# A pooling mixer worked out behind the half groups of a projection, and loads issued from GpSimd's queue, in a two-layer decoder trunk

## The chip, the core and the metric

The kernel runs on one core of one Trainium2 chip. The metric is the device time of one execution in microseconds (us). Below, PE is TensorE, DVE is VectorE, ACT is ScalarE, POOL is GpSimd and SP is SyncE, whose queue issues transfers; L564 is line 564 of the kernel before. The change adds lines, so that the same statement has a number some 3 to 9 higher in the changed kernel (L564 is L567 there, L878 is L881).

## The reference, cut to what matters

Two layers work on 256 tokens of width 2048. A vector c gives, per layer, six sections of conditioning (shift, scale and gate for the mixer and for the feed-forward part), each 2048 wide. Layer 0 has one input projection that feeds an attention with a window and a pooling mixer; both outputs go into one output projection, and a gated feed-forward part follows.

```python
c_act = silu(c)
mod = c_act @ ada_w[layer] + ada_b[layer]          # 6 sections of 2048
h = rms_norm(x, norm_mix_pre) * (1 + sc_m) + sh_m
q, k, v, p = split(h @ w_in)                       # layer 0
a = sliding_window_attention(q, k, v, sinks)
# pooling mixer, 4 groups of 256 channels, windows 2, 4, 8, 16
d = trailing_mean(p, win) - p
bo = (einsum('btgc,gcd->btgd', d, pool_w) + pool_b) * pool_scale
y = concat([a, bo]) @ w_out
x = x + gt_m * rms_norm(y, norm_mix_post)
h = rms_norm(x, norm_ffn_pre) * (1 + sc_f) + sh_f
y = (gelu(conv(h @ w_up_gate)) * (h @ w_up)) @ w_down
x = x + gt_f * rms_norm(y, norm_ffn_post)
```

## The kernel before, in words

All weights stream from memory in pieces of 1 MB. A piece is loaded into one of three slots tagged "w"; ACT copies it, rounded, into an upper half (`whi`, L303), DVE subtracts to get the lower half (`wlo`, L304), each in two instructions of 128x1024, and PE multiplies in three passes (upper by upper, upper by lower, lower by upper: `mm3`, L339 to L341).

The conditioning is worked out in between, in blocks of 128 channels. Blocks of the tables `ada_m` and `ada_dve` take one 1 MB load and one DVE instruction each (L564, a multiply with `c_row` summed along the row, and the short L565). The gate of the mixer (`ada_g`) takes 16 loads and four PE instructions each (L547). The loads of `ada_pe` and `ada_m` alternate between two slots tagged "a" and the "w" slots; all `ada_g` and `ada_dve` loads go to "a" slots. In the kernel before, every load of either tag is issued from SP's queue.

Who does a block when is set by the object `behind` with the generator `ada_gate` (16 steps) followed by the 144 blocks of `ada_dve`. `push()` does one step. `step()` is called with every `load_split` and pushes `pace` steps on average; `PACE_0` sets the pace over the eight parts of the first output projection (two loads each). `need(l, s, b)` pushes until block b of section s is done; it is called by `norm.scale`, which needs the shift and the scale of four channel blocks at a time. The order of `ada_dve` is shift and scale of the feed-forward part of layer 0 block by block, then its gate, then layer 1.

Layer 0 runs so:

- `first_of_all` (L406) does the input projection in four quarters of the inner dimension; in each, five groups of weights (`EV_ORDER`), each with two half groups of 24 matmuls (h = 0, 1). Groups 0 and 1 stay in PSUM; the half groups of groups 2 to 4 are added up in SBUF (`held`, L434). The next quarter's blocks of `ada_m` are pushed by `between`.
- `even_layer` (from L886) then makes keys and queries and works out the pooling mixer: `pool_tile` (L857) forms window sums on DVE, `pool_group` (L874) multiplies by `pool_w` on PE (L878) and scales on DVE (L881). After each of the four groups, `POOL_PUSH` pushes two steps of `behind`, 8 in all. One step of attention (`next(att)`) comes after the first group.
- The output projection runs in two halves, first over the mixer's channels, then over the attention's. The attention is a filler of the first half.
- The feed-forward part starts with `first_halves` (L437): 24 column tiles in two sets of three weight groups; quarters 0 and 1 of the first set, then quarters 0 to 3 of the second set (each group in a quarter is a part of 48 matmuls), then the rest of the first set. `norm.scale` is called ahead of each of the four quarters. After each part, `half_way` pushes one step while fewer than `ADA_0` = 48 are done. The pace of `step()` is 0 here.

An order of instructions on each engine is set by a scheduler at build time, and each engine then runs its own list in order.

Of the kernel before, what the change touches and what calls it, by code (L numbers as in the profile page):

```python
# [38 lines left out]
MARKED = 4  # L39
QUIET = 1  # L40
PACE_0 = (2, 2, 2, 2, 1.5, 1, 1, 0.5)
POOL_PUSH = (2, 2, 2, 2)
EV_ORDER = (0, 1, 2, 3, 4), (3, 4, 2, 0, 1)
ADA_PACE = (0.65, 0.35, 0.2)
SH_M, SC_M, GT_M, SH_F, SC_F, GT_F = range(6)
# [133 lines left out]
def trunk(ctx: ExitStack, tc: tile.TileContext, A, out):  # L179
    nc = tc.nc  # L180
# [113 lines left out]
    behind = Behind()  # L294


    def load(src, shape=(128, NK, 128), tag="w"):
        w = wst.tile(list(shape), F32, name="w", tag=tag, bufs=SLOTS[tag == "a"])
        nc.sync.dma_start(w, src)
        return w  # L300

    def split(src, hi, lo):
# [100 lines left out]
                        between(q, 4 * g + i // 4)  # L403
        return PS

    def first_of_all(norm, between):  # L406


        fixed = [bank((128, 2, T)) for _ in range(4)]
        held = [granule() for _ in range(6)]  # L410
        for q in range(4):
            norm.scale(slice(4 * q, 4 * q + 4))
            for k in range(4 * q, 4 * q + 4):
                norm.tile(k)
            for n, g in enumerate(EV_ORDER[q == 3]):
                W = load_split(A["ev_first"][q, g])
                for h in range(2):
                    stay = g < 2
                    ps = fixed[2 * g + h] if stay else bank((128, 2, T))
                    for k in range(4):  # L420
                        act = norm.tile(4 * q + k)
                        for j in range(2):
                            flags = (k == 0 and j == 0 and not (stay and q), k == 3 and not (stay and q < 3))
                            if (g, h) == (4, 1):
                                mm3(ps[:, j, :], tok(act, j), W(8 + 2 * k, 2), *flags, skip_group_check=True)
                            else:
                                mm3(ps[:, j, :], W(8 * h + 4 * j + k), act, *flags, skip_group_check=True)
                        between(q, 8 * n + 4 * h + k)
                    if not stay:
                        to = held[2 * g - 4 + h]  # L430
                        if q == 0:
                            nc.scalar.activation(to, ps, AF.Copy)
                        else:
                            nc.vector.tensor_tensor(to, ps, to, op=OP.add)  # L434
        return [t[:, j, :] for t in fixed + held for j in range(2)], held[5]
# [391 lines left out]
    def new_mix():  # L827
        M = {}

        def mix(k):  # L830
            if k not in M:
                g = granule(F32R)
                M[k] = g[:, 0, :], g[:, 1, :]
            return M[k]
        return mix
# [48 lines left out]
    def even_layer():  # L884
# [20 lines left out]
        def between(q, g):  # L905
            if q < 3 and g in EARLY:
                next(quarters[q + 1])
            if q < 3 and g == 39:
                drain(quarters[q + 1])
        PS, v = first_of_all(norm, between)  # L910
        kz = key_halves(PS[0:2])
        Q = Copies()
        Q = [Q.copy(ps, scale=q_scale[:, t:t + 1]) for t, ps in enumerate(PS[2:8])]
        for t, ps in enumerate(PS[8:10]):
            nc.scalar.activation(ps, ps, AF.Copy, scale=q_scale[:, 6 + t:7 + t])
            Q.append(ps)
        rec = pool_consts()
        pw = load(A["pool_w"], (128, 4, 2, 256))
        mix = new_mix()
        behind.pace = PACE_0[0]  # L920
        att = behind.fill(attention(Q, kz, v, distances(True), lambda h: sm("sinks", h), lambda t: mix(8 + t)))
        for g in range(4):
            pool_group(g, [pool_tile(g, PS[10 + 2 * g + e], rec) for e in range(2)], pw, mix)
            if g == 0:
                next(att)
            for _ in range(POOL_PUSH[g]):
                behind.push()
        post = Post(0, GT_M, "norm_mix_post0", "up_first0", Norm(0, SC_F, SH_F, "norm_ffn_pre0"))
        for half in range(2):
            if half:  # L930
# [272 lines left out]
```

## Time and profile before

| | us |
|---|---|
| median of 3 runs | 2221.96 |
| lowest and highest run | 2221.46 and 2225.73 |
| the profiled execution's own time | 2221.93 |
| its span | 2220.2 |
| PE busy in it | 2143.8 (97%) |
| DVE busy in it | 1686.2 (76%) |

The span is what the profile records, and the execution's own time is 1.7 us longer. PE is busy for 97% of the span, and the chain of work that ended last lies on PE for 90% of it. PE's time with nothing running is 76 us in all. A busy PE is not one at its peak: an isolated matmul shows its whole length, while back to back matmuls overlap.

### The profile page before, as it was taken

What the parts mean: (1) busy time and instruction counts of PE and PEld (TensorE: products, weight loads), DVE (VectorE), ACT (ScalarE), POOL (GpSimd) and SP (SyncE); (2) the same over time, 40 slices, a digit from 0 to 9 for tenths busy, and PEclk for the clock granted to TensorE, in tenths of its full rate; (3) what the DMA queues carried; (4) which work ended last, traced back from release to release, by engine and by line L of the source; (5) the groups of instructions that cost most, each with busy time, mean ns of one, the idle gap of its engine ahead of it and who ended that gap; (6) DMA issues with size and microseconds to landing.
All of it is one profiled execution on the core that took longest, in us unless ns stands there. A gap on an engine that the chain in (4) does not pass through costs nothing.

```text
span 2220.2 us, 31418 instructions
## 1 busy us (share of the span) xinstructions
PE 2143.8 (97%) x12390; PEld 1857.7 (84%) x12390; DVE 1686.2 (76%) x2533; ACT 1153.6 (52%) x1790; POOL 10.4 (0%) x48
## 2 busy tenths in 40 slices
PE   7888998999999999999899999989999999999998
PEld 5886677997888888888797898878888888888886
DVE  4896798898899899887799867579955665665566
ACT  3345655464555455445576655555545544554453
POOL 1000000000000000000000000000000000000000
PEclk8899998999999999999999999989999999999999
DMA  9987886889889888887387635558855555555553
GB/s 372 348 334 280 322 339 258 328 310 350 308 325 341 331 322 332 330 332 263 135 300 275 229 132 190 190 189 307 319 209 184 188 197 189 190 188 194 188 190 114
DMA packets 81373, 578.42 MB, mean 261 GB/s; under 512 B 9156, under 2 KB 9156, under 8 KB 11464
## 3 DMA queue, kind: packets, MB, share of 16 engines
q1 hardware_dynamic: 81224, 576.40, 70.5%
q8 instruction: 97, 1.59, 0.3%
q14 instruction: 52, 0.43, 0.1%
HBM read 574.27 MB, written 2.10 MB: 260 GB/s over the span
## 4 chain that ended last, share of the span: by engine, by line
PE 90%; DVE 6%; ACT 2%; DMA 1%; issue 1%; SPq 0%; DVEq 0%; ACTq 0%
PE ps L358 28%; PE ps L361 15%; PE ps L340 14%; PE ps L339 14%; PE ps L341 14%; DVE w L564 2%; DVE wlo L304 2%; ACT g L582 1%; PE ps L758 1%; PE ps L547 1%; ACT whi L303 0%; PE ps L795 0%; PE ps L805 0%; DVE x L696 0%; DMA x<-in_x_dram 0%
## 5 line engine op out<-in xcount | busy, mean ns | idle before, releaser
L304 DVE TENSOR_TENSOR wlo<-w,whi 128x1024 fp32r<-128x1024 f32 (+1 forms) x706 | 847.7, 1218 | 314.9 <-PE ps L340 155.6
L303 ACT ACTIVATE whi<-w 128x1024 fp32r<-128x1024 f32 (+1 forms) x706 | 737.4, 1055 | 587.0 <-PE ps L341 281.4
L358 PE MATMUL ps<-g,whi 128*128 128x512 f32 x2736 | 654.4, 391 | 0.0
L358 PEld LDWEIGHTS ps<-g,whi 128*128 128x128 f32 x2736 | 501.9, 188 | 100.5 <-issue 1.2
L340 PE MATMUL ps<-wlo,g 128*128 128x512 f32 (+1 forms) x1152 | 429.1, 373 | 2.2 <-DVE wlo L304 2.2
L339 PE MATMUL ps<-whi,g 128*128 128x512 f32 (+1 forms) x1152 | 428.8, 373 | 0.3 <-ACT g L303 0.2
L341 PE MATMUL ps<-whi,g 128*128 128x512 f32 (+1 forms) x1152 | 428.2, 372 | 0.6 <-DVE g L304 0.6
L564 DVE SCALAR_TENSOR_TENSOR w<-w,c_row 128x2048 f32<-128x2048 f32 x168 | 383.7, 2285 | 3.9 <-DMA w<-in_ada_dve_dram 3.8
L361 PEld LDWEIGHTS ps<-g,wlo 128*128 128x128 f32 x2736 | 350.5, 191 | 13.6
L361 PE MATMUL ps<-g,wlo 128*128 128x256 f32 x2736 | 354.9, 283 | 0.0
L340 PEld LDWEIGHTS ps<-wlo,g 128*128 128x128 f32 x1152 | 217.1, 188 | 42.9 <-DVE wlo L304 4.0
L339 PEld LDWEIGHTS ps<-whi,g 128*128 128x128 f32 x1152 | 216.9, 188 | 40.5 <-issue 1.9
L341 PEld LDWEIGHTS ps<-whi,g 128*128 128x128 f32 x1152 | 216.9, 188 | 38.7 <-DVE g L304 1.5
L339 PE MATMUL ps<-g,whi 128*128 128x256 f32 x800 | 234.9, 297 | 13.7 <-ACT whi L303 7.1
L340 PE MATMUL ps<-g,whi 128*128 128x256 f32 x800 | 235.0, 295 | 0.3 <-DVE g L630 0.3
L341 PE MATMUL ps<-g,wlo 128*128 128x256 f32 x800 | 231.3, 294 | 1.4 <-DVE wlo L304 1.3
L339 PEld LDWEIGHTS ps<-g,whi 128*128 128x128 f32 x800 | 161.2, 203 | 17.3 <-ACT whi L303 8.7
L340 PEld LDWEIGHTS ps<-g,whi 128*128 128x128 f32 x800 | 161.8, 202 | 2.4 <-DVE g L630 2.3
L341 PEld LDWEIGHTS ps<-g,wlo 128*128 128x128 f32 x800 | 160.4, 202 | 2.4 <-DVE wlo L304 2.0
L366 ACT ACTIVATE low<-ps 128x256 f32<-128x256 f32 x156 | 59.5, 381 | 94.8 <-PE ps L361 94.4
L1133 DVE SCALAR_TENSOR_TENSOR z<-low,smalls,z 128x255 f32<-128x255 f32 (+1 forms) x148 | 71.3, 482 | 25.1 <-ACT z L1131 23.5
L1131 ACT ACTIVATE z<-low,smalls 128x256 f32<-128x256 f32 x74 | 44.6, 602 | 84.5 <-DVE low L367 84.5
(195 smaller groups left out, 1173.8 us busy)
## 6 DMA issues: line engine op xcount, KB each, us to landing
w<-in_up_dram SPq DMA_DIRECT2D x148, 1024.0 KB, 4.8
w<-in_ada_dve_dram SPq DMA_DIRECT2D x144, 1024.0 KB, 6.9
w<-in_down_dram SPq DMA_DIRECT2D x88, 1024.0 KB, 4.8
w<-in_up_first_dram SPq DMA_DIRECT2D x28, 1024.0 KB, 7.7
w<-in_ada_m_dram SPq DMA_DIRECT2D x24, 1024.0 KB, 7.5
w<-in_ev_first_dram SPq DMA_DIRECT2D x20, 1024.0 KB, 7.1
w<-in_ada_g_dram SPq DMA_DIRECT2D x16, 1024.0 KB, 4.8
w<-in_ev_out_dram SPq DMA_DIRECT2D x16, 1024.0 KB, 7.8
```

The costliest lines, as they stand in the source:

```text
L303: nc.scalar.activation(hi, src, AF.Copy)
L304: nc.vector.tensor_tensor(lo, src, hi.bitcast(F32), op=OP.subtract)
L339: nc.tensor.matmul(ps, lh, rh, start=first, stop=False, **kw)
L340: nc.tensor.matmul(ps, lh, rl, start=False, stop=False, **kw)
L341: nc.tensor.matmul(ps, ll, rh, start=False, stop=last, **kw)
L358: nc.tensor.matmul(self.ps.rearrange("p a b -> p (a b)"), w(k)[0], act(k).both, start=k == 0, stop=False, skip_group_check=True)
L361: nc.tensor.matmul(self.ps[:, 0, :], w(k)[1], act(k)[0], start=False, stop=k == NK - 1, skip_group_check=True)
L366: nc.scalar.activation(low, self.ps[:, 1, :], AF.Copy)
L547: nc.tensor.matmul(ps[32 * j:32 * j + 32, :], c_rep[:, k, :], w[:, 0, 512 * j:512 * j + 512], start=k == 0, stop=k == NK - 1, tile_positio ...
L564: nc.vector.scalar_tensor_tensor(w, w, 1.0, c_row, op0=OP.mult, op1=OP.mult, accum_out=m)
L1131: nc.scalar.activation(z, pg, AF.Identity, scale=cw(2, f), bias=sm(f"ffn_b{l}", f))
L1133: nc.vector.scalar_tensor_tensor(z[:, lag:], pg[:, :T - lag], cw(2 - lag, f), z[:, lag:], op0=OP.mult, op1=OP.add)
```

## The change

The pooling mixer is worked out inside the last quarter of `first_of_all`: after every half group but the first two a callback `pools` does one `pool_tile`, and after every second one the `pool_group` of the group that came before; the groups come in the order 1, 2, 3, 0, and group 0's `pool_group` comes after the projection. `POOL_PUSH` and its 8 pushes are gone, and nothing takes their place. Every load with tag "a" is issued from GpSimd's queue. `pool_w` is loaded into an "a" slot instead of a "w" slot.

```diff
-POOL_PUSH = (2, 2, 2, 2)
+POOL_ORDER = (1, 2, 3, 0)
...
         w = wst.tile(list(shape), F32, name="w", tag=tag, bufs=SLOTS[tag == "a"])
-        nc.sync.dma_start(w, src)
+        (nc.gpsimd if tag == "a" else nc.sync).dma_start(w, src)
...
-    def first_of_all(norm, between):
+    def first_of_all(norm, between, done):
...
                         between(q, 8 * n + 4 * h + k)
+                    if q == 3 and n:
+                        done(2 * n + h - 2, held)
...
-        PS, v = first_of_all(norm, between)
+        rec = pool_consts()
+        mix = new_mix()
+        pw, ds = [], {}
+
+        def pools(i, held):
+            if i == 0:
+                pw.append(load(A["pool_w"], (128, 4, 2, 256), "a"))
+            g, e = POOL_ORDER[i // 2], i % 2
+            t = 2 + 2 * g + e
+            ds.setdefault(g, []).append(pool_tile(g, held[t // 2][:, t % 2, :], rec))
+            if e == 0 and i:
+                last = POOL_ORDER[i // 2 - 1]
+                pool_group(last, ds[last], pw[0], mix)
+        PS, v = first_of_all(norm, between, pools)
...
-        rec = pool_consts()
-        pw = load(A["pool_w"], (128, 4, 2, 256))
-        mix = new_mix()
+        pool_group(POOL_ORDER[3], ds[POOL_ORDER[3]], pw[0], mix)
         behind.pace = PACE_0[0]
         att = behind.fill(attention(...))
-        for g in range(4):
-            pool_group(g, [pool_tile(g, PS[10 + 2 * g + e], rec) for e in range(2)], pw, mix)
-            if g == 0:
-                next(att)
-            for _ in range(POOL_PUSH[g]):
-                behind.push()
+        next(att)
```

What the scheduler makes of it shows in the lists of the engines. First PE, at the end of the projection, before (`ps_342` is the projection's last bank, L878 the mixer, L757 and L758 the first attention scores, L547 the gate's blocks):

```order
L340 MATMUL ps_342<-g_1492,whi_1745 128x256
L341 MATMUL ps_342<-g_1492,wlo_1746 128x256
L878 MATMUL ps_1855<-pdiff_1842,w_1824 128x256
L878 MATMUL ps_1855<-pdiff_1851,w_1824 128x256
L878 MATMUL ps_1863<-pdiff_1842,w_1824 128x256
L878 MATMUL ps_1863<-pdiff_1851,w_1824 128x256
L757 MATMUL ps_1871<-g_1797,g_1805 128x128
L758 MATMUL ps_1871<-g_1797,g_1805 128x256
L757 MATMUL ps_1886<-g_1797,g_1805 128x128
L758 MATMUL ps_1886<-g_1797,g_1805 128x256
L547 MATMUL ps_1901<-w_1902,c_rep_78 32x512 x4
L547 MATMUL ps_1901<-w_1908,c_rep_78 32x512 x4
```

The same place in the changed kernel (L881 is the mixer, L760 and L761 the scores, L550 the gate's blocks, L798 the transposes of the attention's weights):

```order
L340 MATMUL ps_350<-g_1500,whi_1865 128x256
L341 MATMUL ps_350<-g_1500,wlo_1866 128x256
L881 MATMUL ps_1970<-pdiff_1898,w_1600 128x256
L881 MATMUL ps_1978<-pdiff_1898,w_1600 128x256
L760 MATMUL ps_1997<-g_1951,g_1959 128x128
L761 MATMUL ps_1997<-g_1951,g_1959 128x256
L881 MATMUL ps_1970<-pdiff_1947,w_1600 128x256
L881 MATMUL ps_1978<-pdiff_1947,w_1600 128x256
L760 MATMUL ps_2012<-g_1951,g_1959 128x128
L761 MATMUL ps_2012<-g_1951,g_1959 128x256
L550 MATMUL ps_2042<-w_2043,c_rep_78 32x512 x4
L798 MATMUL ps_2055<-ident_93,p_2000 128x128
```

Twelve of the sixteen mixer matmuls now stand between the projection's matmuls, and four behind them; two steps of the gate stand between the first scores and the output projection, where eight stood.

Second DVE, in the feed-forward part, ahead of the casts (L629, L632) of the second quarter's activations. Before, from the third conditioning block after the first quarter's casts:

```order
L564 SCALAR_TENSOR_TENSOR w_3486,mod04_124<-w_3486,c_row_79 128x2048
L304 TENSOR_TENSOR wlo_3530<-w_3527,whi_3529 128x1024
L565 TENSOR_TENSOR mod04_124<-mod04_124,smalls_76 128x1
L304 TENSOR_TENSOR wlo_3534<-w_3527,whi_3533 128x1024
L564 SCALAR_TENSOR_TENSOR w_3585,mod03_123<-w_3585,c_row_79 128x2048
L565 TENSOR_TENSOR mod03_123<-mod03_123,smalls_76 128x1
L304 TENSOR_TENSOR wlo_3592<-w_3589,whi_3591 128x1024
L629 CAST g_3500<-h_3498 128x256
L629 CAST g_3508<-h_3506 128x256
```

In the changed kernel, from the fifth block on (L608 makes the scale `s` that the casts' input waits for):

```order
L567 SCALAR_TENSOR_TENSOR w_3462,mod04_124<-w_3462,c_row_79 128x2048
L304 TENSOR_TENSOR wlo_3584<-w_3577,whi_3583 128x1024
L568 TENSOR_TENSOR mod04_124<-mod04_124,smalls_76 128x1
L567 SCALAR_TENSOR_TENSOR w_3466,mod03_123<-w_3466,c_row_79 128x2048
L304 TENSOR_TENSOR wlo_3642<-w_3639,whi_3641 128x1024
L568 TENSOR_TENSOR mod03_123<-mod03_123,smalls_76 128x1
L567 SCALAR_TENSOR_TENSOR w_3470,mod04_124<-w_3470,c_row_79 128x2048
L568 TENSOR_TENSOR mod04_124<-mod04_124,smalls_76 128x1
L608 SCALAR_TENSOR_TENSOR s_2028<-mod04_124,smalls_76 128x4
L632 CAST g_3488<-h_3486 128x256
L567 SCALAR_TENSOR_TENSOR w_3474,mod03_123<-w_3474,c_row_79 128x2048
L633 TENSOR_TENSOR g_3488<-h_3486,g_3488 128x256
```

Four blocks and eight lower halves stand between the first casts of quarters 0 and 1 before, seven blocks and ten lower halves in the changed kernel, an eighth block stands behind the first cast, and the scale `s` stands behind the seventh.

Third POOL, in the first 200 us; a piece of the difference, with - before and + in the changed kernel (L860 and L863 clear the pads of the window sums, L748 and L751 clear the tiles of the keys):

```order
 L239 AFFINE_SELECT dist<-dist 128x256
-L860 MEMSET pd 128x16
+L299 DMA w<-in_ada_pe_dram 128x2048
 L242 AFFINE_SELECT dist<-dist 128x256
-L748 MEMSET g 128x512 x2
-L860 MEMSET pd 128x16 x7
+L299 DMA w<-in_ada_m_dram 128x2048 x12
+L299 DMA w<-in_pool_w_dram 128x2048
+L299 DMA w<-in_ada_g_dram 128x2048
+L863 MEMSET pd 128x16 x7
+L751 MEMSET g 128x512 x2
+L299 DMA w<-in_ada_g_dram 128x2048 x15
```

The clears stand behind loads that wait for a free slot, and later in the list `pool_w`'s slot has to be free for the gate's second load.

## Rows read from the trace of the kernel before

**Rows 1.** The page, busy time of each engine: share of the span, instructions.

```profile
PE 2143.8 (97%) x12390; PEld 1857.7 (84%) x12390; DVE 1686.2 (76%) x2533; ACT 1153.6 (52%) x1790; POOL 10.4 (0%) x48
```

**Rows 2.** Busy time by stretch: us, busy and count by engine, PE clock, DMA share, GB/s.

```profile
core 0: us, PE busy (x) PEld busy (x) DVE busy (x) ACT busy (x) POOL busy (x), PEclk, DMA share, GB/s
35.00:153.00 118.00, 103.64 (x742) 100.06 (x742) 104.85 (x140) 43.29 (x55) 0.00 (x0) 0.88 0.91 350
...
215.50:287.00 71.50, 70.19 (x383) 48.36 (x382) 49.85 (x138) 47.54 (x132) 1.90 (x4) 1.00 0.86 323
```

**Rows 3.** Timeline of PE from the projection's end to the output projection's start.

```profile
185.11 0.28 PE L340 MATMUL ps<-g,whi 128*128 128x256 f32 x1
185.23 0.28 PE L341 MATMUL ps<-g,wlo 128*128 128x256 f32 x1
185.35 1.89 PE L878 MATMUL ps<-pdiff,w 128*128 128x256 f32 x8
187.08 0.38 PE L757 MATMUL ps<-g 128*128 128x128 f32 x2
...
192.63 1.25 PE L878 MATMUL ps<-pdiff,w 128*128 128x256 f32 x4 [2.22 <-DVE pdiff L871]
...
213.69 1.06 PE L547 MATMUL ps<-w,c_rep 128*32 128x512 f32 x8
214.69 0.66 PE L805 MATMUL ps<-pt,g 128*64 128x256 f32 x4
...
215.50 0.50 PE L339 MATMUL ps<-whi,g 128*128 128x512 f32 x1
```

**Rows 4.** Busy time by stretch, from the first cast to the fourth quarter's.

```profile
352.75:447.81 95.06, 92.74 (x743) 90.83 (x742) 80.85 (x106) 43.31 (x56) 0.00 (x0) 0.98 0.83 324
```

**Rows 5.** Waits of SP's queue over the span: us in total, times, longest.

```profile
SPq L299 <- DVE mod L565: 157.0, 38, 9.9
SPq L299 <- DVE w L564: 133.2, 42, 6.7
```

**Rows 6.** Waits of DVE from 35 to 153 us, same columns.

```profile
DVE wlo L304 <- ACT whi L303: 7.4, 3, 2.7
DVE g L434 <- PE ps L341: 4.7, 5, 1.1
```

**Rows 7.** The gate's blocks, L547, from 185 to 216 us: count, ns min/median/max.

```profile
L547 PE MATMUL ps<-w,c_rep x64: 592/617/1062, 188.5 to 214.2; 128*32 128x512 f32 x64
```

**Rows 8.** Timeline of ACT, the last scaling of the first attention weights.

```profile
195.23 0.80 ACT L781 ACTIVATE p<-p,st 128x128 f32<-128x128 f32 x2 [0.18 <-DVE st L776]
```

**Rows 9.** The page, transfers: count, size, median us from issue to landing.

```profile
w<-in_ada_dve_dram SPq DMA_DIRECT2D x144, 1024.0 KB, 6.9
```

**Rows 10.** Timeline of DVE in the feed-forward part's first quarters.

```profile
367.53 1.22 DVE L304 TENSOR_TENSOR wlo<-w,whi 128x1024 fp32r<-128x1024 f32 x1
368.67 0.15 DVE L565 TENSOR_TENSOR mod<-mod,smalls 128x1 f32<-128x1 f32 x1
368.74 1.22 DVE L304 TENSOR_TENSOR wlo<-w,whi 128x1024 fp32r<-128x1024 f32 x1
369.87 2.29 DVE L564 SCALAR_TENSOR_TENSOR w<-w,c_row 128x2048 f32<-128x2048 f32 x1
372.08 0.08 DVE L564 DVE_READ_ACCUMULATOR w<-w,c_row 128x1 f32 x1
...
428.46 0.29 DVE L629 CAST g<-h 128x256 fp32r<-128x256 f32 x1 [5.28 <-ACT h L627]
...
447.81 0.29 DVE L629 CAST g<-h 128x256 fp32r<-128x256 f32 x1 [1.42 <-ACT h L627]
```

**Rows 11.** Busy time by stretch of 5 us, around the feed-forward part's start.

```profile
350.00:355.00 5.00, 3.69 (x15) 3.52 (x16) 2.83 (x11) 3.37 (x9) 0.00 (x0) 0.50 0.00 0
355.00:360.00 5.00, 5.00 (x35) 5.00 (x35) 5.00 (x7) 5.00 (x7) 0.00 (x0) 0.77 0.39 123
360.00:365.00 5.00, 5.00 (x44) 5.00 (x43) 5.00 (x6) 0.03 (x1) 0.00 (x0) 1.00 0.93 333
```

## The prediction

> **What bounds the kernel now.** I read the page's busy times first, then the busy time by stretch, then the timelines of PE and DVE where the change acts, then the waits. PE is busy for 2143.8 of 2220.2 us [rows 1], so a change gains only by what PE does not do, and each microsecond that PE is made to stand costs one at the end. Beyond the feed-forward part's first quarters of layer 0 the change adds and removes no PE work, so I look at four stretches. From 35 to 153 us (three quarters of the projection) PE is not the bound: DVE is busy for 104.85 of 118 us and the transfers are at a share of 0.91 [rows 2]. From 185.35 to 215.50 us the pooling mixer, the gate and the first attention step run by turns, with visible gaps on PE [rows 3]. From 215.5 to 287 us PE is busy for 70.19 of 71.5 us at the full clock [rows 2]. In the feed-forward part's first quarters PE is busy for 92.74 and DVE for 80.85 of 95.06 us [rows 4]: DVE has 14 us to spare there, no more.
>
> **Part 1: the queue split, 0 to 153 us.** SP waited 157.0 and 133.2 us over the span for conditioning slots [rows 5], and weight loads stood behind those waits. On POOL's queue the waits hold up nobody's weights. In this stretch DVE has 24 blocks and 31 lower halves to do before quarter 3 in either kernel, so its own 105 us stay; what can go is its idle time, 118 - 104.85 = 13 us, of which 7.4 us are waits for upper halves and 4.7 us waits for PE [rows 2, 6]. The transfers bound the gain from the other side: 0.91 of the time is taken already [rows 2]; at full share the stretch would be 118 x 0.91 = 107 us, 11 us less. The list of the changed kernel has two more blocks done ahead of quarter 1, which uses the time when DVE idled, and one block ahead of the very first casts, which has to wait for its load. Nothing makes the stretch longer but that one block, 2.3 us. Bounds -11 and +2; I take -5, about the middle, since the waits for PE stay and those for upper halves lie where transfers are dense.
>
> The Trainium skill, DMA: Bandwidth & Descriptors, section "Issuing engines are not separate DMA queues", says that transfers started by different engines share the same 16 DMA engines, and that starting them from several saves only issue time. The share of 0.91 agrees with that as far as it goes. By that rule alone this part would be 0 instead of -5, and the sum below 2237.
>
> **Part 2: the mixer, 153 to 287 us.** The 30.15 us from 185.35 to 215.50 hold this PE work, by distances of starts: 32 rows of the mixer at (187.08 - 185.35) / 8 = 0.216 us, 6.9 us [rows 3]; 64 rows of the gate [rows 7] at (214.69 - 213.69) / 8 = 0.125 us, 8.0 us; two sets of scores, six transposes and one set of value products, about 4.4 us. That is 19.3 us of work and 10.8 us of stall. The work does not go away: the mixer's 6.9 us lengthen the last quarter, where matmuls follow each other every 0.12 us [rows 3] and PE had no gap, and six of the eight gate steps move into the output projection's first half, where PE has none either [rows 2]. Only the stall can go. What is left of it, from the lists: the mixer's matmuls in the last quarter wait for DVE, whose list there also holds the lower halves of the next weights; adding up that list with the durations before gives waits of about 0.4, 0.4 and 1.8 us. Then the transposes follow the second scores with only one gate step (1.0 us) between, while before the weights of the second head were ready at 195.23 + 0.8 = 196.0 us [rows 8], 7.5 us after its scores, behind which the gate starts at 188.5 [rows 7]. DVE and ACT are emptier now, so I take 5 us of waiting. The gate's second load starts only when `pool_w`'s slot is free, after the last mixer matmul, and takes 6.9 us at the median [rows 9]; it lies beside the same 5 us. Left: 7 us, gain 10.8 - 7 = 4. Bounds: -9 if only the softmax chain's first 2 us stay, +2 if the last quarter's DVE list is late throughout. The clears that moved behind loads on POOL wait for slots freed before 153 us, so they cost nothing; if such a load were late, the first window sum would be too, and with it the mixer: that is inside the +2.
>
> **Part 3: the eight pushes, 350 to 460 us.** This is the term that decides. Before, 8 pushes in the mixer, 16 and 8 in the two halves of the output projection make 32: 16 gate steps and 16 blocks. Without the 8 the count is 24, 8 blocks, which is just what quarter 0 of the feed-forward part needs (scale and shift of four channel blocks). Quarter 1 needs 32, and three parts push only three: five more are forced by `need` at once. Quarter 3 needs 48, and 44 are there: four are forced. Counting the two lists from the first cast of quarter 0 to the first cast of quarter 3, DVE has 16 blocks and 31 lower halves before, and 26 blocks and 34 lower halves now. A block costs 2.28 us (2.21 from 369.87 to 372.08, and 0.07 for its L565: 368.67 to 368.74), a lower half 1.13 to 1.14 us [rows 10]. Added: 10 x 2.28 + 3 x 1.14 = 26.2 us. DVE had 95.06 - 80.85 = 14.2 us to spare [rows 4], so even a DVE that never idles starts quarter 3 at least 12 us later. It will idle: 5.28 us of the spare time is one wait ahead of quarter 2 [rows 10] that a late quarter 1 does fill, but the rest are waits for upper halves whose weights were still in flight. Ten more MB also have to come through two slots in bursts, 6.9 us each from issue to landing [rows 9]; 95.06 us at 324 GB/s are 30.8 MB [rows 4], and 41 MB at the 350 GB/s of the densest long stretch [rows 2] are 117 us, 22 us more. Bounds 12 and 24; I take 18, the middle. The first piece of it shows at quarter 1: seven blocks instead of four ahead of `s`, and one inside the casts, about 10 to 13 us of PE standing.
>
> Where PE stands, the clock falls: 0.50 (1.2 GHz) at 350 to 355 us after PE waited for the norm, 0.77 in the next 5 us, 1.00 (2.4 GHz) after [rows 11]. About 5 us at half speed cost 1.5 us beyond the wait itself, once, at quarter 1. From quarter 3 on both kernels have 48 steps done and the same pace, so nothing is won back: behind it PE is the bound.
>
> **Part 4: nothing.** Issuing 180 transfers from POOL instead of SP costs no compute: POOL is busy for 10.4 us in all [rows 1]. In layer 1 POOL's clears for the keys stand behind the 112th block's load; if that is late, attention there starts a few us later, beside PE work. I count 0, at most 2.
>
> **Sum.** Against the profiled execution's own 2221.93 us (0.03 under the median of 2221.96): -5 - 4 + 18 + 1.5 = +10.5, so 2232.4 us, about 0.5% slower.
>
> **Rivals.** *A, the queue split frees the projection.* Not slower: if DVE never idled from 35 to 153 us and the start were 3 us earlier, part 1 would be -16, and the time 2221.4. From -11 on the whole is within 0.2%, at -15.5 it is level with before. For it: SP's 290 us of slot waits [rows 5]. Against: a DMA share of 0.91 [rows 2], which leaves 11 us. *B, the blocks come at the floor.* Part 3 at 12, part 1 at -9, part 2 at -9 and a clock term of 1: 2217, faster by just over 0.2%. For it: POOL's loads start the moment a slot is free, so the forced blocks find their data. Against: three ends at once. *C, POOL's loads are held up by DVE.* Each load on POOL's queue would start only when the DVE instruction under way ends, on average half of 1.2 to 2.3 us, 0.8 us for each of 26 blocks in the feed-forward stretch; where DVE then waits in a row (the ten added ones) 8 us, so 2240.4. For it: DVE is 85% busy there [rows 4]. Against: before, no load was issued from POOL, so no row shows it. *D, the split gains nothing* and the rest holds: 2237.4.
>
> The Trainium skill, SBUF — State Buffer, section "SBUF: two separate sides", warns of a case like C: descriptors for a transfer issued from GpSimd are written by GpSimd through a port pair that certain VectorE instructions hold for their whole length. The page names copies and casts in a two-port mode, not two-input instructions such as L564 and L304; the casts here are 0.29 us long, so by its letter the cost would be small. No row before shows it.
>
> **How the numbers follow.** A measurement of this kernel can tell about 0.2%, here 2217.5 to 2226.4 us. My own case (2227 to 2239) gets 0.50, C 0.12, D 0.08: slower 0.70. A and milder mixtures of its gain with a cheap part 3 get 0.18: same. B and beyond get 0.12: faster. Ends for the range: low -9 - 6 + 12 = -3, 2218; high 0 + 2 + 18 + 2 = +22, 2244. That leaves B's far side and C with a bad part 3 out, about 2 in 10. The likeliest sign is slower, and its own range is 2227 to 2244.
>
> **What would show it.** Right: DVE shows seven L567 in a row of turns with L304 ahead of the second casts, PE waits there for about 10 us for the casts' input, with a clock near 0.5 behind it, and the fourth quarter's first cast comes 12 to 20 us later against the first than the 95.06 us before; the output projection's first matmul comes about 10 us earlier against quarter 3's scale, and PE's stretch from 215.5 on grows by six gate steps. Wrong: the stretch to quarter 3's scale is over 10 us shorter than before (A); or the forced blocks pass with PE waiting for under 5 us; or POOL's DMA rows land far later than 6.9 us (C).

## The result, and the profile after

The changed kernel takes 2284.70 us, the median of 6 runs (2281.19 to 2293.63), beside 2221.71 us for the kernel before: a ratio of 1.0292, 95% interval 1.0266 to 1.0317. It is 63 us slower. The forecast was 2232.4 us, 10.5 us slower, with a range that ended at 2244. The sign held and the size did not.

The profiled execution has a span of 2285.6 us, 65.4 us more than before. PE does the same work; the time between it grew from 76 to 134 us, as the busy times of the page show (before: [rows 1]):

```profile
PE 2151.6 (94%) x12390; PEld 1867.0 (82%) x12390; DVE 1684.4 (74%) x2533; ACT 1144.9 (50%) x1790; POOL 103.8 (5%) x225
```

To place the 65.4 us I count the weight matmuls on PE (three passes of `mm3` and their like, 11,328 in every kernel here) and compare when the same one starts. The table gives that for the kernel before, and by how many us each other kernel is later (minus: earlier). It is worked out from the traces; the runs e1 to e12 come below. Quarters are counted from 0 in it, so that quarter 3 is the fourth.

```
                        before  change   e1     e2     e3     e5     e7     e9    e11    e12
output proj. begins      215.5    -8.7  +5.7   +3.2   -7.6   -3.4   +7.8   -7.6  -11.2   -0.8
feed-forward 0 begins    353.1    -6.2  +6.4   +1.8   -9.0   -3.0  +10.6   -3.5   -7.4   -0.8
2,101st: its quarter 3   453.1   +28.1 +22.9  +22.4  +12.2   -4.1  +14.4  +23.9   -8.1   -2.1
2,701st                  549.9   +25.5 +20.2  +23.9  +13.8   -4.2  +13.0  +22.8   -8.2  +19.4
4,501st                  883.2   +54.9 +42.0  +23.9  +13.8   -4.2  +13.0  +22.8   -8.2  +49.4
6,001st: layer 1        1183.9   +66.7 +49.2  +23.9  +13.9   -4.2  +14.1  +24.2   -8.3  +65.5
last                    2211.3   +65.3 +48.1  +23.9  +14.0   -4.2  +14.4  +24.5  -10.0  +63.5
```

So the changed kernel is 6.2 us ahead where the feed-forward part begins, loses 34.3 us in that part's first four quarters, 29.4 us between the 2,701st and 4,501st weight matmul, and 11.8 us around layer 1's attention. My sum had nothing behind the fourth quarter.

**The second quarter.** The timeline of DVE in the changed kernel, ahead of the scale `s` (start, duration, engine, line; in brackets the idle time before it and what ended it):

```profile
373.37 2.28 DVE L567 SCALAR_TENSOR_TENSOR w<-w,c_row 128x2048 f32<-128x2048 f32 x1
...
375.58 1.22 DVE L304 TENSOR_TENSOR wlo<-w,whi 128x1024 fp32r<-128x1024 f32 x1
...
381.48 2.29 DVE L567 SCALAR_TENSOR_TENSOR w<-w,c_row 128x2048 f32<-128x2048 f32 x1 [4.61 <-DMA w<-in_ada_dve_dram]
...
384.01 0.16 DVE L608 SCALAR_TENSOR_TENSOR s<-mod,smalls 128x4 f32<-128x4 f32 x1
```

The last forced block waits 4.61 us for its load, and `s` is ready at 384.01. PE and its clock there (the timeline of PE, then the busy time by stretch with PE's clock as the third number from the end):

```profile
384.89 1.14 PE L627 MATMUL ps<-ident,g 128*128 128x128 f32 x4 [18.44 <-ACT h L630]
```

```profile
384.00:389.00 5.00, 3.59 (x15) 3.13 (x16) 4.22 (x11) 2.15 (x4) 1.17 (x2) 0.50 0.59 211
389.00:394.00 5.00, 5.00 (x29) 5.00 (x28) 3.62 (x5) 1.02 (x2) 0.53 (x1) 0.59 0.73 234
```

PE stands 18.44 us, and then has some 8 us at its lower level (0.50 is 1.2 GHz, and a mean of 0.59 makes about 4 of the second row's 5 us), where I had put 5.

**All four quarters.** The busy time by stretch of the changed kernel, from the first cast of quarter 0 to the first cast of quarter 3, and the wait of DVE in it that is largest in total (us in total, times, longest):

```profile
346.50:475.16 128.66, 97.51 (x748) 94.76 (x746) 106.34 (x139) 49.78 (x62) 13.36 (x25) 0.87 0.86 337
```

```profile
DVE w L567 <- DMA w<-in_ada_dve_dram: 17.6, 9, 4.6
```

The stretch is 33.6 us longer than the 95.06 before [rows 4], where I had named 12 to 20. DVE has 25.5 us more to do in it (106.34 - 80.85); my lists had given 26.2. But its idle time, of which I had counted 14.2 us as spare, did not shrink: it is 22.3 us, and 17.6 of it are waits for the blocks' own loads. In e2 (below), where those loads stay on SP's queue and the waits for them come to 1.0 us, DVE still idles for 16.5 of 114.07 us.

**Behind the fourth quarter.** The same weight work fills 575 to 885 us before and about 600 to 940 us in the changed kernel. By stretch, first before, then the changed kernel:

```profile
575.00:885.00 310.00, 310.00 (x1697) 270.37 (x1696) 279.57 (x383) 161.46 (x223) 0.00 (x0) 1.00 0.87 326
```

```profile
600.00:940.00 340.00, 322.53 (x1710) 277.18 (x1710) 306.91 (x421) 154.21 (x224) 28.63 (x54) 0.98 0.91 346
```

PE never stood there before. Now it stands 17.5 us in the open, and its busy time is 12.5 us longer for nearly the same matmuls. The blocks in that stretch, L564 before and L567 after (min/median/max in ns):

```profile
L564 DVE SCALAR_TENSOR_TENSOR w<-w,c_row x42: 2280/2284/2294, 576.4 to 882.9; 128x2048 f32<-128x2048 f32 x42
```

```profile
L567 DVE SCALAR_TENSOR_TENSOR w<-w,c_row x54: 2282/2287/2295, 599.9 to 911.7; 128x2048 f32<-128x2048 f32 x54
```

Twelve more blocks for the same weights, 12 x 2.28 = 27.4 us of DVE, which is the growth of its busy time (306.91 - 279.57 = 27.3). DVE's busy share is 0.90 in both stretches (279.57 / 310 and 306.91 / 340). So the stretch grew about as much as DVE's work in it. The twelve blocks' loads had to come too: the transfers went from 326 to 346 GB/s. The waits (us in total, times, longest) of the changed kernel from 600 to 940 us show it on the way to PE:

```profile
ACT whi L303 <- DMA w<-in_up_dram: 92.1, 37, 7.1
...
DVE w L567 <- DMA w<-in_ada_dve_dram: 17.3, 10, 3.4
...
PE ps L361 <- DVE wlo L304: 10.5, 10, 2.9
```

Before, ACT waited 20.2 us for those weights and PE for no lower half. What stood on the way shows in the chain of work that ended last, by line, as shares of the two stretches (before, then the changed kernel; "issue" is time in which an engine waited for nothing that the profile shows):

```profile
by line: PE ps L358 51.8%; PE ps L361 27.2%; PE ps L340 7.0%; PE ps L341 7.0%; PE ps L339 7.0%
```

```profile
by line: issue 25.5%; DMA w<-in_ada_dve_dram 20.8%; DVE w L567 13.9%; DMA w<-in_up_dram 11.3%; DVE wlo L304 9.5%; PE ps L358 2.8%; ACT whi L303 2.1%; PE ps L340 1.9%; PE ps L341 1.8%; DVE low L367 1.7%; PE ps L339 1.6%; DVE z L1142 1.5%; PE
```

Before, it lay on PE alone. Now the loads of blocks (20.8%), the loads of `up` weights (11.3%) and DVE's multiplies and lower halves (13.9% and 9.5%) all lie on it, and for a quarter of it the profile names nothing. So DVE's work did not act alone here: loads stood on the way too, and the early blocks waited for theirs (17.3 us above).

Why are there twelve more? Not because of pushes: from the fourth quarter on both kernels have done 48 and go at the same pace, and e2 and e3, which lack the same pushes, have the list of the kernel before from there on. The lists of DVE tell it. Blocks that stand ahead of the n-th lower half:

```
n                 97   116   142   180   214   240   264   288   311   336
before            44    53    60    72    82    89    98   105   112   120
change            36    52    62    81    93   103   118   126   130   130
e2, e3 no pushes  36    50    60    72    82    89    98   105   112   120
e1 queue alone    44    56    66    85    97   107   122   130   130   130
e7, e9 held       44,36 53,50 60    71    80    87    95   101   107   114
e12 crowded       44    53    65    85    99   109   121   131   140   151
```

The program asks for the blocks at the same places, but the list that the build makes has up to 21 more of them ahead of the same lower half (126 beside 105 at the 288th). My theory from here: the build places an instruction where its operands can be there by its own reckoning; on SP's queue a block's load stood behind the weights' loads, and on GpSimd's queue it stands behind nothing but its slot. The lists were there to be read before the run; I had counted them only up to the fourth quarter's first cast.

**Layer 1's attention.** The same thing at one place, in the changed kernel (DVE, then PE):

```profile
1220.63 2.29 DVE L567 SCALAR_TENSOR_TENSOR w<-w,c_row 128x2048 f32<-128x2048 f32 x1 [3.55 <-DMA w<-in_ada_dve_dram]
...
1222.85 0.55 DVE L782 TENSOR_SCALAR p<-p,st 128x128 f32<-128x128 f32 x2
```

```profile
1223.27 1.36 PE L798 MATMUL ps<-ident,p 128*128 128x128 f32 x4 [4.31 <-DVE p L782]
```

A block stands ahead of the softmax's scaling and waits for its load; the scaling, ready to go, waits behind it, and PE 4.31 us behind that. In e7 and e9, with the same queue and the list held, the loss around there is 1.1 and 1.4 us beside 11.8, so the order makes most of it, and not the clears that stand behind loads in POOL's list.

### The profile page after: what moved, and what is told of

The parts are those of the page before. It is cut to its first block, busy times and chain, and to the rows that moved or that the text cites. A ratio compares the mean times of both kernels' runs of the same rounds, so it can differ in the third digit from the quotient of the medians.

```text
span 2285.6 us, 31557 instructions
## 1 busy us (share of the span) xinstructions
PE 2151.6 (94%) x12390; PEld 1867.0 (82%) x12390; DVE 1684.4 (74%) x2533; ACT 1144.9 (50%) x1790; POOL 103.8 (5%) x225
## 4 chain that ended last, share of the span: by engine, by line
PE 65%; DMA 13%; DVE 10%; issue 9%; ACT 2%; POOL 0%; SPq 0%; DVEq 0%; POOLq 0%; ACTq 0%
PE ps L358 20%; PE ps L361 10%; PE ps L340 10%; PE ps L339 10%; PE ps L341 10%; DMA w<-in_ada_dve_dram 7%; DVE w L567 5%; DVE wlo L304 3%; DMA w<-in_ev_first_dram 2%; DMA w<-in_up_dram 2%; DMA w<-in_ada_g_dram 2%; ACT whi L303 1%; ACT g L585 1%; DMA w<-in_ada_m_dram 1%; DMA g<-in_c_row_dram 0%
## 5 line engine op out<-in xcount | busy, mean ns | idle before, releaser
L567 DVE SCALAR_TENSOR_TENSOR w<-w,c_row 128x2048 f32<-128x2048 f32 x168 | 383.8, 2287 | 59.6 <-DMA w<-in_ada_dve_dram 54.1
L361 PE MATMUL ps<-g,wlo 128*128 128x256 f32 x2736 | 358.8, 283 | 10.6 <-DVE wlo L304 10.5
L299 POOL DMA_DIRECT2D w<-in_ada_dve_dram x144 | 76.5, 531 | 1304.1 <-DVE w L567 1170.4
```

The source lines that it names most:

```text
L299: (nc.gpsimd if tag == "a" else nc.sync).dma_start(w, src)
L361: nc.tensor.matmul(self.ps[:, 0, :], w(k)[1], act(k)[0], start=False, stop=k == NK - 1, skip_group_check=True)
L567: nc.vector.scalar_tensor_tensor(w, w, 1.0, c_row, op0=OP.mult, op1=OP.mult, accum_out=m)
```

## The experiments

Two theories. *Order*: the loss is the missing pushes (in the first quarters) plus what the queue split does to DVE's list. *Pushes*: all of it is the missing pushes and their echo. A third, *the queue itself*: transfers on a second queue share the bandwidth and delay weights, whatever the list.

**e1, the queue split alone** (on the kernel before):

```diff
-        nc.sync.dma_start(w, src)
+        (nc.gpsimd if tag == "a" else nc.sync).dma_start(w, src)
```

> The kernel before with one line changed: loads with tag a issued from GpSimd's queue. In the list of DVE the build then places the conditioning blocks earlier behind the fourth quarter of layer 0's feed-forward part: 85 blocks ahead of the 180th lower half instead of 72, 130 ahead of the 311th instead of 112. Theory (order): that crowding costs PE the 27 us that the change lost between its first 2700 and 4500 weight matmuls, and the loads and clears on GpSimd's queue the 12 us lost around layer 1's attention; with nothing lost at the pushes it gives about 2222 + 27 + 12 = 2261, 2250 to 2270. Rival (pushes): all 63 us are the late blocks and their echo, and the queue split costs nothing: 2216 to 2224. My forecast had -5 for it: 2217.

Measured: 2284.40 us, ratio 1.0279 (1.0242 to 1.0316): 63 us slower by itself, with no step moved and no push missing. The rival falls, and so does my forecast's -5; the order theory's 2261 (up to 2270) was too low as well. The profiled run took 2270.03 us and the three others 2283 to 2287, so the table's +48.1 leaves some 14 us of the median unplaced.

**e2, the pushes removed alone** (on the kernel before): 

```diff
-POOL_PUSH = (2, 2, 2, 2)
+POOL_PUSH = (0, 0, 0, 0)
```

> The kernel before with POOL_PUSH at zero, all loads on SP's queue. The list of DVE then has 8 blocks fewer ahead of the first quarter of layer 0's feed-forward part and the same number from the fourth on. Theory (order): the loss at the second to fourth quarter alone, +20 to +34 us, nothing lost behind it, and the eight gate steps no longer stand ahead of the output projection, up to -4: 2238 to 2256, with 2246 the likeliest. Rival (pushes cause everything): about 2222 + 75 = 2297, because the mixer's gain of 12 us is missing here. Forecast's term: +18 + 1.5, 2241.

Measured: 2245.70 us, 1.0112 (1.0086 to 1.0138), 24.5 us slower. From the start of the feed-forward part to its fourth quarter it loses 22.4 - 1.8 = 20.6 us, and 1.5 us behind it. PE's stand at the second quarter:

```profile
387.38 1.14 PE L624 MATMUL ps<-ident,g 128*128 128x128 f32 x4 [12.91 <-ACT h L627]
```

That is the forced blocks as forecast, 10 to 13 us, and there is no echo behind them.

**e3, the change without the queue split:** e1's line undone in the changed kernel.

> The changed kernel with every load issued from SP's queue again: the mixer is moved and the eight pushes are gone, nothing else. Theory (order): the mixer's gain of 12 us as far as the output projection's start, of which 6 are lost again in it, and the pushes' loss of 20 to 34: 2232 to 2252. Rival (pushes cause everything): 2280 or more. Rival (the mixer's gain in the changed kernel needs the queue split, because the clears and pool_w come earlier from it): no gain, so it equals the run with the pushes removed to 3 us.

Measured: 2234.66 us, 1.0064 (1.0041 to 1.0086). It is 11 us better than e2, which lacks the same pushes: moving the mixer gains, without the split. Both rivals fall.

**e4, e3 with the eight pushes back:**

```diff
         next(att)
+        for _ in range(8):
+            behind.push()
```

> The run before this one with eight pushes put back, behind the first attention step and ahead of the output projection. The list of DVE then agrees with the kernel before from the output projection on, to 1 block. Theory (order): only the mixer's gain is left, 6 to 12 us: 2210 to 2216. Rival (the eight gate steps that stood between mixer and output projection were the cover for the softmax, so that putting them back returns the gap): 2218 to 2222. Forecast's term for the mixer alone: -4, 2218.

Measured: 2227.42 us, 1.0028 (1.0012 to 1.0043). A miss: the second quarter's stall is gone, but the output projection loses 16 us (7.7 ahead at its start, 8.4 behind at its end). One stand of PE there is in the timeline:

```profile
280.73 1.30 PE L798 MATMUL ps<-ident,p 128*128 128x128 f32 x4 [6.05 <-ACT p L784]
```

The other 10 us I have not placed. Pushes are not free where they are put.

**e5, e3 with the pushes in the projection's last quarter:** one `behind.push()` ahead of each `pool_tile` in `pools`.

> The changed kernel with every load on SP's queue and eight pushes put back, one with each window sum in the projection's last quarter, where transfers have a share of 0.73 and not 0.83 as in the output projection's first half. Theory: the earlier variant with the pushes ahead of the output projection lost 13 us there because 8 more MB of gate loads stood in SP's queue between the projection's last weights and the output projection's; here they are issued 30 us earlier, so the mixer's gain of 11 us stays: 2209 to 2215. Rival (the steps themselves fill the last quarter, where PE has no gap, and their loads hold up the quarter's weights): 2219 to 2230.

Measured: 2218.92 us, 0.9993 (0.9974 to 1.0012). Over the theory's range and at the edge of the rival's. The pushes cost 8.5 us less than in e4, but the output projection begins 4.2 us later than in e3: the gate steps now stand ahead of it, as the rival had it.

**e6, e3 with the pushes by a higher pace:**

```diff
-PACE_0 = (2, 2, 2, 2, 1.5, 1, 1, 0.5)
+PACE_0 = (2, 2, 2, 2, 2.5, 2, 2, 1.5)
```

> The changed kernel with every load on SP's queue and eight pushes put back by a higher pace in the output projection's second half (2.5, 2, 2, 1.5 for 1.5, 1, 1, 0.5). Theory: the first half then runs as in the run with the mixer alone (gain 7 us at its end against before, 11 against the run with the pushes removed); the second half has 16 blocks instead of 8 in 55 us, DVE was busy for 57 of 63 us there before, so it takes up to 8 x 2.28 = 18 us less the 6 spare: 2215 to 2228, 2221 the likeliest. Rival (the half is bound by its weights' transfers): as the theory's low end.

Measured: 2224.38 us, 1.0031 (1.0017 to 1.0045), as the theory had it: 11.6 us ahead at the output projection's start, 5.8 us behind at its end. PE waits 13.94 us for DVE ahead of the next norm's first matmul, with DVE busy for 17.84 of the 20 us from 330 on, five blocks among it.

**e7, e1 with the list held:** each block's multiply is kept behind the last lower half that precedes it in the program; loads stay on GpSimd's queue.

```diff
+            with ExitStack() as order:
+                if name == "ada_dve" and len(lows) >= 1:
+                    order.enter_context(tc.issue_after(lows[-1].ins))
-            nc.vector.scalar_tensor_tensor(w, w, 1.0, c_row, ...)
+                nc.vector.scalar_tensor_tensor(w, w, 1.0, c_row, ...)
```

> The kernel before with loads of tag a issued from GpSimd's queue, and each block's multiply kept behind the lower half that precedes it in the program, by an order on DVE alone. DVE's list then has the same number of blocks as the kernel before ahead of every lower half up to the 169th, and at most 7 fewer later (107 for 112 at the 311th), where the queue split alone had up to 25 more. Theory (order): the 21 us that the split alone lost from 575 to 885 us go away, and most of the 13 us of the quarters before: 2222 + 6 to 2222 + 30. Rival (the second queue itself: block loads on it share the transfers with weights as soon as a slot is free): the loss stays, since the slots come free at the same pace: 2260 to 2285.

Measured: 2234.56 us, 1.0065 (1.0042 to 1.0088). 50 of e1's 63 us are gone, though the queue is the same. The stretch, in e1 and then in e7:

```profile
600.00:925.00 325.00, 309.99 (x1654) 267.10 (x1654) 291.97 (x401) 152.33 (x222) 25.35 (x48) 0.99 0.89 341
```

```profile
575.00:900.00 325.00, 325.00 (x1771) 283.11 (x1770) 278.01 (x380) 170.55 (x233) 20.08 (x38) 1.00 0.83 311
```

PE stands nowhere. The queue itself is not the cause there; the order is. Some 13 us against the kernel before are left; the table has 10.6 of them where the feed-forward part begins.

**e8, e5 with only the 12 loads of `ada_m` in slots "a" issued from GpSimd's queue:**

```diff
-            w = load(A[name][n], (128, 1, D), ATAG[n % 2] if name == "ada_m" else "a")[:, 0, :]
+            w = load(A[name][n], (128, 1, D), ATAG[n % 2] if name == "ada_m" else "a",
+                     nc.gpsimd if name == "ada_m" and n % 2 == ATAG.index("a") else nc.sync)[:, 0, :]
```

> The run of pushes in the last quarter, with the 12 loads of ada_m that go to slots of tag a issued from GpSimd's queue, and all others from SP's. Theory: the queue split alone began the projection 6.6 us late, because the first loads went ahead of x, and stood level at 145 us; with the first loads on SP's queue the catching up of 7 us is left: 5 to 7 us under the run of pushes in the last quarter. Rival (the catching up is only the late start's own stall made good, as the wait for transfers is the same): within 2 us of it.

Measured: 2216.40 us, 0.9978 (0.9966 to 0.9989), 2.5 us under e5, which lies between theory and rival and is not clear of the noise. But its start was not earlier: the first weight matmul starts at 45.6 us, in e5 at 37.3. With the very first loads on SP's queue the start is late all the same, so their going ahead of x is not the main cause. DVE's timeline in e8 shows what is:

```profile
29.45 0.29 DVE L601 TENSOR_SCALAR diag<-ident,r 128x128 f32<-128x128 f32 x1
39.62 2.29 DVE L568 SCALAR_TENSOR_TENSOR w<-w,c_row 128x2048 f32<-128x2048 f32 x1 [9.88 <-DMA w<-in_ada_m_dram]
...
42.37 0.16 DVE L541 TENSOR_TENSOR mod<-tr,smalls 128x4 f32<-128x4 f32 x1
```

The first block stands in the list ahead of the add for the first shift (L541), and DVE waits 9.88 us for its load. In e5 that add comes at 34.13. Once more an instruction placed too early. In e1 that add is 1.0 us later than in the kernel before, and a block between it and the first casts waits 5.94 us for its load.

**e9, the changed kernel with the list held**, for `ada_m` and `ada_dve` (the edit of e7):

> The changed kernel (mixer moved, queue split, eight pushes gone), with every block's multiply kept behind the lower half that precedes it in the program, by an order on DVE alone. Theory (two causes: the order of DVE's list that the split brings, and the missing pushes): the 47 us that the hold gave back on the queue split alone go here too, and the start's block no longer stands ahead of the first casts: 2285 - 47 = 2238, and up to 7 less: 2230 to 2242; PE without a gap of note from 600 us to 900 us. Rival (in the changed kernel the loss there is a late echo of the missing pushes): above 2265.

Measured: 2245.24 us, 1.0114 (1.0086 to 1.0141), 39.5 us under the changed kernel and 3 over the theory's range; PE is busy for 300.00 of the 300 us from 600 on. The rival falls: no echo of the pushes there.

**e10, e9 with the pushes of e5:** 

> The run before this one with eight pushes, one with each window sum in the projection's last quarter: both features of the change are kept and both suspected causes are taken away. Theory: the missing pushes cost 24 us alone, and the pushes in the last quarter gave back 16 of them in the kernel on SP's queue (2235 to 2219): 2214 to 2228. Rival (the second queue costs something of its own in the dense stretches, 10 us at the mixer and the output projection as the queue split with the list held showed): 2226 to 2236.

Measured: 2230.28 us, 1.0046 (1.0029 to 1.0062). Both causes are out and 54 of 63 us are back, but the time lies in the rival's range and 2 us over the theory's: 11 us more than e5, which has no split. PE's timeline in e10 behind the projection:

```profile
199.61 1.06 PE L552 MATMUL ps<-w,c_rep 128*32 128x512 f32 x8 [1.42 <-DMA w<-in_ada_g_dram]
206.05 1.93 PE L552 MATMUL ps<-w,c_rep 128*32 128x512 f32 x8 [3.44 <-DMA w<-in_ada_g_dram]
```

These gate loads are on GpSimd's queue now; in e5 and e11, where they are on SP's, PE does not wait for them. The waits are 4.9 us; the output projection begins 3.7 us later than in e5 (0.4 late beside 3.4 ahead). Another 4.7 us are lost in the feed-forward part's first four quarters (from 4.4 to 9.1 us behind e5), and I have no cause for them.

**e11, e8 with the multiplies of `ada_m` held** (the edit of e7, for `ada_m`):

> The run with 12 loads of ada_m on GpSimd's queue and the pushes in the last quarter, with the multiplies of ada_m kept behind the lower half that precedes them in the program. In its list the first block stood ahead of the short add that the first shift needs, and DVE waited 9.9 us for that block's load with PE behind it. Theory: the start comes 8 us earlier and a part of it lasts: 2208 to 2214. Rival (the transfers bound the projection, so a start 8 us earlier is level again at 145 us): 2215 to 2218, as before.

Measured: 2213.86 us, 0.9970 (0.9960 to 0.9980). The start is right again (38.2 us) and a part of it lasts, 2.5 us against e8, as the theory had it at its upper end; the two intervals overlap. This version beats both kernels: 7 us under the kernel before, 71 under the changed one.

**e12, the kernel before with its list crowded by a higher pace**, all loads on SP's queue:

```diff
-ADA_MID = 0.75
+ADA_MID = 1.75
...
-ADA_PACE = (0.65, 0.35, 0.2)
+ADA_PACE = (1.0, 0.35, 0.2)
```

> The kernel before, all loads on SP's queue, with the pace of blocks raised in layer 0's feed-forward part (ADA_MID 1.75 for 0.75, ADA_PACE's first number 1.0 for 0.65), so that DVE's list has as many blocks ahead of each lower half as with the queue split: 65, 80, 85, 90, 99, 109, 121, 131 ahead of the 142nd, 169th, 180th, 192nd, 214th, 240th, 264th, 288th (split alone: 66, 77, 85, 89, 97, 107, 122, 130). Theory (crowding of blocks, whatever the queue): PE loses about 21 us from 575 to 885 us as with the split: 2236 to 2246. Rival (crowding costs only where the loads also overtake the weights on a queue of their own): 2216 to 2228.

Measured: 2285.33 us, 1.0291 (1.0269 to 1.0313), 39 us over the theory's range; the rival falls. Crowding alone, without any second queue, costs as much as the whole change: 30.0 us from the 2,701st to the 4,501st matmul, beside 29.4 in the changed kernel, and more around that, since the raised pace begins earlier and lasts longer than the split's lead. Its stretch, two of its waits from 575 to 925 us, and the chain that ended last, by line, as shares of the stretch:

```profile
575.00:900.00 325.00, 305.56 (x1607) 259.66 (x1607) 300.25 (x400) 142.49 (x205) 0.00 (x0) 1.00 0.88 348
```

```profile
ACT z L1131 <- DVE low L367: 89.8, 21, 4.3
...
PE ps L358 <- ACT whi L303: 14.8, 20, 0.8
```

```profile
by line: DVE wlo L304 30.2%; DVE w L564 27.9%; PE ps L340 8.0%; PE ps L341 7.6%; PE ps L339 6.8%; ACT whi L303 6.0%; DVE low L367 3.9%; ACT z L1131 3.2%; issue 3.0%; DVE z L1138 1.9%; DVE mod L565 0.9%; DVE g L687 0.9%; DVE g L304 0.4%; DVE
```

ACT stands at L1131, the start of the feed-forward part's convolution, for a sum that DVE has not made yet (L367), so its next upper half is late, and PE waits for that. The chain lies on DVE's lower halves and multiplies for 58% and on no load among the lines shown, although the transfers, too, are busier than before (348 GB/s beside 326). DVE's share is 300.25 / 325 = 0.92: DVE's list is enough to make PE stand. In the changed kernel loads lie on the chain beside DVE (20.8% and 11.3%, above); how the loss there divides between the two these runs do not part, and e7 takes away both at once.

## Why the prediction was wrong

- **Part 1, -5 (-11 to +2): held.** The scale of the last quarter comes at 150.26 us instead of 153.01: -2.75, although the start was late: the block ahead of the first casts, which I had priced at 2.3 us, waits another 3.53 us for its load, and the first weight matmul is 4.4 us late. By the quarter's own first weight matmul, the 721st, only 1.0 us is gained, and in e1, the split alone, 1.5 us are lost. e11, with the start mended, is 4.5 us ahead there. Rival A, a freed projection, has nothing for it. The Trainium skill, DMA: Bandwidth & Descriptors, section "Issuing engines are not separate DMA queues", said 0 by its rule; the changed kernel lies between that and my -5, and e1 nearer to the rule.
- **Part 2, -4 (-9 to +2): held in the sum.** From that scale to the start of the feed-forward part the changed kernel gains another 6.2 - 2.75 = 3.5 us. Its parts were both smaller than I had them: 5.9 us up to the output projection's start, where I had 10, and 2.5 of it lost again behind that, where I had six gate steps. e3 against e2 shows 11 us on SP's queue: there the eight gate steps are gone from between the old mixer's parts, and, as I read it, the waits that they covered stand open, so the move is worth more.
- **Part 3, +18 and 1.5 for the clock (12 to 24): the forced blocks held, the size did not.** The changed kernel loses 34.3 us in these quarters, 10 over the upper bound. The count was right (26 blocks and 34 lower halves), but I had let DVE's spare time pay for a part of it, all 14.2 us at the lower bound and some 8 at 18, and none of it did: DVE idled more. e2 gives 20.6 us, near the forecast, by luck: it has 7 blocks more and not 10, and they cost more than their 16.7 us of DVE. The pushes alone are not my ten blocks, then: the split adds 6 blocks and 3 lower halves by itself and loses 22.9 - 6.4 = 16.5 us there (e1), for which I had no term.
- **Part 4, 0 at most 2, and the sentence "From quarter 3 on both kernels have 48 steps done and the same pace, so nothing is won back: behind it PE is the bound": this is the step that failed.** The count of steps is equal, the place of their instructions is not. From the fourth quarter to the end the changed kernel loses 65.3 - 28.1 = 37.2 us. In its place the runs show DVE's list: with the split it has up to 21 blocks more ahead of the same weights, and PE waits behind them and their loads. Held back to the program's order, the same queue loses next to nothing from the fourth quarter on (e7: 14.4 us behind there and at the end; e9: 23.9 and 24.5). I read [rows 4] with its 14 us to spare as a limit for the first quarters only, and took the rest of the program for covered, where DVE was at 0.90.
- **The sum** of the trace, -2.75 - 3.5 + 34.3 + 37.2 = 65.3, has the first two terms within their bounds, the third 10 us over its own, and the one that I put at nothing larger than all of them. No rival had a loss behind the fourth quarter either. (The range's low end, -3, is 2219 by its own sum, not 2218; nothing hangs on it.)
- **Rival C, loads held up by DVE: fell.** Every issue of a block's load on POOL takes nearly the same time, DVE at 90% or not (min/median/max in ns), and the loads land in 6.0 us at the median, before 6.9 [rows 9]:

```profile
L299 POOL DMA_DIRECT2D w<-in_ada_dve_dram x144: 530/530/637, 276.6 to 1652.8; - x144
```

  The hold-up that the Trainium skill warns of, SBUF — State Buffer, section "SBUF: two separate sides", shows in no run here (the longest issue of any load on POOL's queue is 0.70 us); by its letter it should not: instructions with two inputs, as these are, stand there as holding the ports only against GpSimd's reads.

Shown by removal and by addition: the order (e7, e9 take it away, e12 crowds the list of the kernel before) and the pushes (e2 takes them out, e4 to e6 put them back). Argued, not shown: how the build comes to that order. Open: how the loss divides between DVE's work and the loads, 14 us of e1's median, some 7 us of e10 against e5, and 10 us of e4.

## What to carry to other kernels

Where a build orders the instructions, the queue that a load is issued from is an input to that order: one changed line put up to 25 more blocks ahead of the same lower half (e1). As I read it, a load that seems free early pulls its consumer ahead, here on an engine that was busy for 0.90 of the time. So count the new lists against the old to the end of the program, on every engine about as busy, not only around the edit. And background work that is dropped from one place is asked for at another: look for the next place that needs its count.

## What the runs showed that I had not expected

- Idle time of DVE beside a full PE was not room. Twelve more multiplies of 2.28 us lengthened a stretch by 30 us and left its idle time as it was (30.4 us before, 33.1 after); in the four quarters of e2 16.7 us of added work lengthened the stretch by 19.0. In e12 DVE reached 0.92 with PE standing 19.4 of 325 us; in e7, at 278.01 / 325 = 0.86, PE stood nowhere.
- Keeping the blocks' multiplies in program order on DVE, with nothing else changed, is worth 50 us (e1 to e7); the queue that is left in e7 costs 13.
- Issuing a 1 MB load takes 0.53 us on POOL and 0.33 us on SP. Whether it lands later goes both ways: blocks of `ada_dve` take 6.0 us at the median on POOL's queue and 6.9 on SP's in the kernel before, but in the changed kernel, which has loads of `ada_m` on both, those take 7.8 us on POOL's and 6.5 on SP's.
